# A hybrid decoder trunk on one core: small float32r products put ahead of float32 ones within a batch, and an early first activation

## The chip, the cores and the metric

The kernel runs on one core of a Trainium2 chip. The metric is the device time of one execution in microseconds (us); lower is better. Engines are named as the profile names them: PE is TensorE's matrix unit, PEld its weight loads, DVE is VectorE, ACT is ScalarE, POOL is GpSimd, SP issues the DMAs.

## The reference

Two layers over 528 tokens (16 learned meta tokens and 512 real ones) of width 1024, in float32. Cut to what matters here:

```
for l in range(DEPTH):                          # DEPTH = 2
    proj = rms_norm(h, norm1_g[l]) @ w_in[l]    # z, xbc, dt, q, k, v, gate logits
    y_ssd = ssd_mixer(z, xbc, dt, ...)          # conv, silu, chunked state-space scan, gated group norm
    y_attn = sliding_window_attention(q, k, v, ...)   # window 128, meta keys, sinks
    merged = g_ssd * (y_ssd @ w_ssd_down[l]) + g_attn * (y_attn @ w_attn_down[l])
    h = h + merged @ w_o[l]
    h = h + square(relu(rms_norm(h, norm2_g[l]) @ w_mlp_up[l])) @ w_mlp_down[l]
return h[:, 16:]
```

## The kernel before

Everything is held transposed, with features on the 128 partitions and tokens along the free dimension. Each large matrix product ("dense", L545) works through 128x128 weight tiles. For accuracy a float32 value is split into a high and a low float32r part (whi and wlo for weights, hnh and hnl for the normalised rows), and three float32r products replace one float32 product: high by high, low by high, high by low. These dense products have 264, 266 or 512 columns and fill most of PE's time.

Besides them there is a large number of small products. Those of attention (L1064) are scores (k2h and k2l by q, two pairs of products at a time) and probabilities by values (ar by vt or vm): both are float32r. Between the two, attention transposes its probabilities (cst by at, L442), which is a float32 operation on PE. All other small products are float32: the state-space chunks (L1228: transposes cst by xb, then btk by xdd, xdt by gm, st by xb), the norms (cst by zs, one column each; cst by rg) and the rotary norms (cst by au, two columns).

The small work is written as generators. Each "yield" ends a stage and names what the next stage needs: "ps" is a free PSUM bank, "pe" says only that the stage issues products, "ar" is a buffer of probabilities. A planner (class Flow) keeps an estimated clock for every engine while the program is being built. After every second dense product it calls "tick" (L265). If the last batch of small products is at least GAP = 3600 ns of its clock ago (the flag open_), tick may issue products; stages that use only DVE, ACT, POOL or SP may be issued at any time. It goes through the queues w, post, misc, tail, chunk, attn in this order and takes the first stage that is ready by its estimates. A stage taken is written into the program at once, and each engine executes its instructions in the order written. So the order of the instructions on each engine is what the planner decides, and the estimated clock has no other effect on the chip.

At the start, SP loads the first parameters, the first row block of h, two weight tiles of v (wraw, 512 KB each), the weights of dt (rawdt), and then the other rows. ACT scales h into hgh, casts the three weights into wvh, and PE's first products wait for these casts. ACT's function table is loaded by an instruction that the compiler puts ahead of ACT's first activation.

Of the kernel before, what the change touches and what calls it, by code (L numbers as in the profile page):

```python
# [9 lines left out]
F32 = mybir.dt.float32  # L10
F32R = mybir.dt.float32r
I32 = mybir.dt.int32
AF = mybir.ActivationFunctionType
# [4 lines left out]
P = 128  # L18
# [62 lines left out]
class Ring:  # L81
# [5 lines left out]
    def at(self, k=1):  # L87
        return sorted(self.free)[k - 1]
# [8 lines left out]
class Task:  # L97
# [3 lines left out]
    def at(self, flow):  # L101

        t = self.ready
        for k, n in self.needs.items():
            if k == "if":
                if not n():
                    return INF
            elif k == "after":
                if not all(x.done for x in n):
                    return INF  # L110
                t = max([t] + [x.end for x in n])
            elif k == "data":
                aps = n()
                if aps is None:
                    return INF
                t = max(t, flow.there("pe", (), aps))
            elif k == "bank":
                t = max(t, flow.rings["ps"].at(n))
            elif k != "pe":
                t = max(t, flow.rings[k].at(n + (flow.SPARED if k == "ps" else 0)))  # L120
        return t


class Flow:
# [52 lines left out]
    def there(self, e, outs, ins):  # L177

        t = 0.0
        for aps, out in ((ins, False), (outs, True)):  # L180
            for ap in aps:
                bank = ap.space == PSUM
                p0, p1, f0, f1 = self.box(ap)
                for log in (self.written, self.read) if out or bank else (self.written,):
                    for q0, q1, g0, g1, at, e_ in log.get(ap.tensor.name, ()):

                        if e_ != e if bank and e_ else False:
                            hit = True
                        else:
                            hit = (out or log is self.written) and q0 < p1 and p0 < q1 and g0 < f1 and f0 < g1  # L190
                        if hit:
                            t = max(t, at + self.HOP.get((e_, e), 130.0))
        return t
# [71 lines left out]
    def tick(self):  # L265


        begin = self.t["pe"]
        open_ = begin - self.batch >= self.GAP
        for _ in range(24):  # L270
            if self.busy():
                break
            now = self.t["pe"]
            calm = max(self.t["v"], self.t["s"]) - now < self.CALM
            for t, q in self.active():
                if not open_ and any(k in ("pe", "ps", "bank") for k in t.needs):
                    continue
                if (calm or q is not self.queues["attn"]) and t.at(self) <= now:
                    self.step(t, q)
                    break  # L280
            else:
                break
        if self.t["pe"] > begin:
            self.batch = self.t["pe"]

    def wait_any(self):

        best = None
        for t, q in self.active():
            at = t.at(self)  # L290
            if at < INF and (best is None or at < best[0]):
                best = (at, t, q)
        assert best is not None, "nothing can go on"
        self.step(best[1], best[2])
# [68 lines left out]
def hybrid_trunk_kernel(ctx: ExitStack, tc: tile.TileContext, h0, params, consts, rope, wdt, w, out,  # L363
# [7 lines left out]
    sm = ctx.enter_context(tc.tile_pool(name="sm", bufs=2))  # L371
# [5 lines left out]
    S = Engine(F, "s", nc.scalar)  # L377
    G = Engine(F, "g", nc.gpsimd)
# [12 lines left out]
    class Slot:  # L391
# [12 lines left out]
        def free(self, at=None):  # L404
            F.rings[self.kind].free[self.j] = max(F.end, F.t["pe"] if at is None else at)
# [8 lines left out]
    def unit(name, dt=F32):  # L414
        return un.tile([P, 4, UW], dt, name=name, tag="u")
# [17 lines left out]
    def mm(o, lhsT, rhs, start=True, stop=True):  # L433
        n = Engine.size(rhs)
        if rhs.dtype == F32R and n >= 256:
            cost = n / 2.4
        else:
            cost = max(n, 128) * 4 / 2.4 * (0.66 if o.shape[0] == 64 else 1.0)
        F.run("pe", cost, [o], [lhsT, rhs], PE.matmul(out=o, lhsT=lhsT, rhs=rhs, start=start, stop=stop))  # L439

    def transpose(o, in_, k=P):
        F.run("pe", 108.0 if in_.shape[1] > 64 else 60.0, [o], [in_], PE.transpose(out=o, in_=in_, identity=C("ident", k)[:, :k]))  # L442
# [246 lines left out]

    h = Rows("h", KD)  # L690
    F.dma(par[:, 0, 0:KD], params[:, 0, 0:KD])
    few = CCOL["low"][0]
    wvt.open(0)
    tasks_ = [x for x, q in F.active()]
# [38 lines left out]
    for l in range(depth):  # L733
# [174 lines left out]
        for c in range(5):  # L908
            ps = banks[c]
# [154 lines left out]
        def attention(n, kv):  # L1064
# [29 lines left out]
            def score(i):  # L1094
                ps = Slot("ps")
                for x in range(2):
                    mm(ps.t[:, :kw], q2[:, i, :], k2[x][:, kv, k0:k0 + kw], start=(x == 0), stop=(x == 1))
                return ps

            def top(i, ps):  # L1100
                col = (4 * a + i) * 2 + hb
                V.tensor_tensor_reduce(out=pt[i], in0=ps.t[:nq, :nk], in1=mask,
                                       scale=rqk[:nq, n, col:col + 1], scalar=sk[:, i:i + 1],
                                       op0=ALU.add, op1=ALU.max, accum_out=mx[:nq, i:i + 1])
                ps.free()

            for i in range(0, 4, 2):
                yield {"ps": 2}
                two = [score(i), score(i + 1)]
                yield  # L1110
                top(i, two[0])
                top(i + 1, two[1])
# [13 lines left out]
            def piece(p):  # L1126

                o, kk, cc = pieces[p]
                need = {"ps": 1, "ar": 1}
                if not po:  # L1130
                    need["ps"], need["po"] = 2, 1
                yield need
                if not po:
                    po.append(Slot("ps"))
                    turn.append(Slot("po"))
                s_, pp = Slot("ar"), Slot("ps")
                if kk < P <= nq:

                    for i in range(4):
                        transpose(pp.t[0:32, i * nq:(i + 1) * nq], pt[i][:, o:o + 32], nq)  # L1140
                    if p == len(pieces) - 1:
                        p_.free()
                    yield
                    h_ = slice(s_.j * 1024, s_.j * 1024 + 4 * nq)
                    S.copy(ar[0:32, h_], pp.t[0:32, :4 * nq])
                    yield
                    V.tensor_tensor(out=ar[32:64, h_], in0=pp.t[0:32, :4 * nq], in1=ar[0:32, h_], op=ALU.subtract)
                    pp.free()
                    yield {"pe": 1}
                    mm(po[0].t[:, :4 * nq], vm[:, kv].rearrange("p x d -> p (x d)"), ar[:, h_],  # L1150
                       start=(p == 0), stop=(p == len(pieces) - 1))
                    s_.free()
                    return
                for i in range(4):
                    transpose(pp.t[:kk, i * nq:(i + 1) * nq], pt[i][:, o:o + kk], nq)
                if p == len(pieces) - 1:
                    p_.free()
                yield
                ph, pl_ = (ar[:kk, s_.j * 1024 + z:s_.j * 1024 + z + 4 * nq] for z in (0, 512))
                S.copy(ph, pp.t[:kk, :4 * nq])  # L1160
                yield
                V.tensor_tensor(out=pl_, in0=pp.t[:kk, :4 * nq], in1=ph, op=ALU.subtract)
                pp.free()
                yield {"pe": 1}
                for x, r in enumerate((ph, pl_)):
                    mm(po[0].t[:, :4 * nq], (vt[:, cc - 1, kv] if cc else vm[:kk, kv]).rearrange("p x d -> p (x d)"), r,
                       start=(p == 0 and x == 0), stop=(p == len(pieces) - 1 and x == 1))
                s_.free()


            live = [piece(p) for p in range(len(pieces))]
            wait, t = {}, 0
            started = 1
# [30 lines left out]
        def put_attention(qt, a):  # L1204
            F.put("misc", q_rms(qt, a))
            for n in range(c_first, 5):
                for kv in (2 * a, 2 * a + 1):
                    att.append(F.put("attn", attention(n, kv)))
# [4 lines left out]
        ar = unit("ar", F32R).rearrange("p r t -> p (r t)")  # L1213
# [580 lines left out]
```

## Time and profile before

| | us |
|---|---|
| median of 3 runs (2354.28, 2356.80, 2356.81) | 2356.8 |
| the profiled execution, its own time | 2351.39 |
| its span, first to last instruction | 2349.5 |
| PE busy in the span | 2322.6 |
| POOL busy | 1327.6 |
| DVE busy | 1186.7 |
| ACT busy | 1027.7 |

The profiled execution is a fourth execution of the same program; 1.9 us of its time lie outside its span. The four executions lie 5.4 us apart. Busy time is the union of the engine's instructions, so for PE it also holds time in which products run slowly.

### The profile page before, as it was taken

Reading aid. Unit: us, or ns where it says so; the run is one execution under the profiler, and the core shown is the slowest. Engines: PE = TensorE matmul, PEld = TensorE weight load, DVE = VectorE, ACT = ScalarE, POOL = GpSimd, SP = SyncE. Lnnn points to the kernel's source line nnn. Section 1 sums busy time; section 2 is a strip of 40 time slices with the busy share of each in tenths; the row PEclk is TensorE's granted clock in tenths of the full one; section 3 lists DMA queues with packets and bytes.
Section 4 is the critical chain, followed back from the end, with each engine's and each line's share of the span. In section 5 each row is a group of like instructions: output and inputs, shape, how many; then the busy total and the mean of one; then the engine's idle time right before and its main releaser. Section 6 shows DMA issues by size and latency. Waiting matters only on the chain.

```text
span 2349.5 us, 41761 instructions
## 1 busy us (share of the span) xinstructions
PE 2322.6 (99%) x16038; PEld 2129.6 (91%) x16038; DVE 1186.7 (51%) x2511; ACT 1027.7 (44%) x2007; POOL 1327.6 (57%) x1733
## 2 busy tenths in 40 slices
PE   8999999999999999999999999999999999999999
PEld 8899999999999999999998888999887888888887
DVE  7687688888422322122146876888873223222121
ACT  5455566666422333223244555656563223423221
POOL 6555545566555555555557555565575555555554
PEclk9999999999999999999999999999999999999999
DMA  4233334433443322222243333333434433222222
GB/s 167 85 93 103 106 105 116 109 93 99 136 165 114 132 81 91 90 91 91 97 141 99 104 103 109 112 104 104 116 104 154 148 113 135 90 99 90 99 98 99
DMA packets 133588, 257.41 MB, mean 110 GB/s; under 512 B 16470, under 2 KB 66318, under 8 KB 133390
## 3 DMA queue, kind: packets, MB, share of 16 engines
q1 hardware_dynamic: 133390, 254.75, 34.5%
q8 instruction: 127, 2.08, 0.4%
q14 instruction: 71, 0.58, 0.1%
HBM read 232.03 MB, written 17.33 MB: 106 GB/s over the span
## 4 chain that ended last, share of the span: by engine, by line
PE 92%; DVE 4%; ACT 1%; POOL 1%; issue 1%; DMA 1%; SPq 0%; ACTq 0%; DVEq 0%; POOLq 0%
PE ps L439 90%; PE ps L442 3%; DVE rqs L356 1%; DVE at L356 1%; DVE xh L356 0%; POOL wlo L356 0%; DVE xb L356 0%; DMA gm<-ac_dram 0%; ACT gm L356 0%; ACT whi L356 0%; DVE raw L356 0%; DVE ar L356 0%; DVE gm L356 0%; DVE qa L356 0%; SPq L232 0%
## 5 line engine op out<-in xcount | busy, mean ns | idle before, releaser
L356 POOL TENSOR_TENSOR wlo<-wraw,whi 128x256 fp32r<-128x256 f32 x1272 | 988.7, 809 | 747.1 <-ACT whi L356 732.9
L356 ACT CAST whi<-wraw 128x1024 fp32r<-128x1024 f32 x340 | 355.6, 1046 | 725.0 <-PE ps L439 692.1
L439 PE MATMUL ps<-hnh,whi 128*128 128x266 f32 (+2 forms) x1984 | 371.7, 305 | 0.0
L439 PE MATMUL ps<-hnl,whi 128*128 128x266 f32 (+2 forms) x1984 | 369.5, 305 | 0.0
L439 PE MATMUL ps<-hnh,wlo 128*128 128x266 f32 (+2 forms) x1984 | 365.6, 304 | 0.0
L439 PEld LDWEIGHTS ps<-hnl,whi 128*128 128x128 f32 x1984 | 293.0, 189 | 13.4
L439 PEld LDWEIGHTS ps<-hnh,wlo 128*128 128x128 f32 x1984 | 291.6, 189 | 13.2
L439 PEld LDWEIGHTS ps<-hnh,whi 128*128 128x128 f32 x1984 | 292.0, 189 | 12.6 <-issue 0.3
L356 DVE SCALAR_TENSOR_TENSOR h<-ps,h 128x264 f32<-128x264 f32 (+1 forms) x120 | 62.1, 518 | 324.4 <-PE ps L439 324.4
L439 PE MATMUL ps<-hgh,wlo 128*128 128x264 f32 (+1 forms) x832 | 165.0, 320 | 0.3 <-POOL wlo L356 0.3
L439 PE MATMUL ps<-hgl,whi 128*128 128x264 f32 (+1 forms) x832 | 164.5, 319 | 0.4 <-DVE hgl L356 0.4
L439 PE MATMUL ps<-hgh,whi 128*128 128x264 f32 (+1 forms) x832 | 164.1, 319 | 0.0
L439 PE MATMUL ps<-hidl,whi 128*128 128x264 f32 (+1 forms) x768 | 152.6, 320 | 0.0
L439 PE MATMUL ps<-hidh,whi 128*128 128x264 f32 (+1 forms) x768 | 152.5, 320 | 0.0
L439 PE MATMUL ps<-hidh,wlo 128*128 128x264 f32 (+1 forms) x768 | 152.5, 320 | 0.0
L356 DVE SCALAR_TENSOR_TENSOR tmp<-ps,rbc 128x264 f32<-128x264 f32 (+1 forms) x96 | 49.3, 515 | 183.7 <-PE ps L439 162.3
L439 PEld LDWEIGHTS ps<-hgh,wlo 128*128 128x128 f32 x832 | 128.6, 190 | 11.5 <-POOL wlo L356 0.5
L439 PEld LDWEIGHTS ps<-hgl,whi 128*128 128x128 f32 x832 | 128.5, 189 | 11.6 <-DVE hgl L356 0.6
L439 PEld LDWEIGHTS ps<-hgh,whi 128*128 128x128 f32 x832 | 128.7, 190 | 11.2
L439 PE MATMUL ps<-y,whi 128*128 128x264 f32 (+1 forms) x768 | 137.0, 320 | 0.0
L439 PEld LDWEIGHTS ps<-hidl,whi 128*128 128x128 f32 x768 | 118.8, 188 | 11.1
L439 PEld LDWEIGHTS ps<-hidh,wlo 128*128 128x128 f32 x768 | 118.7, 188 | 11.1
(217 smaller groups left out, 3904.0 us busy)
## 6 DMA issues: line engine op xcount, KB each, us to landing
wraw<-w_dram SPq DMA_DIRECT2D x344, 512.0 KB, 3.2
gm<-ac_dram SPq DMA_DIRECT2D x64, 256.0 KB, 5.0
et<-ac_dram SPq DMA_DIRECT2D x128, 64.0 KB, 4.7
t<-au SPq DMA_DIRECT2D x48, 66.0 KB, 2.8
h<-h_dram SPq DMA_DIRECT2D x8, 264.0 KB, 4.7
at<-rope_dram SPq DMA_DIRECT2D x4, 528.0 KB, 4.8
y_dram<-xb SPq DMA_DIRECT2D x4, 528.0 KB, 5.2
yr<-y_dram SPq DMA_DIRECT2D x8, 264.0 KB, 4.5
```

Of the source, the lines that this page charges most:

```text
L356: inst = fn(*a, **k)
L439: F.run("pe", cost, [o], [lhsT, rhs], PE.matmul(out=o, lhsT=lhsT, rhs=rhs, start=start, stop=stop))
L442: F.run("pe", 108.0 if in_.shape[1] > 64 else 60.0, [o], [in_], PE.transpose(out=o, in_=in_, identity=C("ident", k)[:, :k]))
```

## The change

It has two parts. First, tick no longer takes the first ready stage. It looks at all ready stages and takes the one of lowest rank: rank 0 is a stage without products, 1 is a stage with float32r products only, 2 a stage that has float32r products and the transposes of attention, 3 a stage of float32 products. Attention's stages carry a mark "r" for this, which has no other use. Second, a one-column activation on a zeroed tile z is written ahead of everything else on ACT.

```diff
             now = self.t["pe"]
             calm = max(self.t["v"], self.t["s"]) - now < self.CALM
+            best = None
             for t, q in self.active():
-                if not open_ and any(k in ("pe", "ps", "bank") for k in t.needs):
-                    continue
-                if (calm or q is not self.queues["attn"]) and t.at(self) <= now:
-                    self.step(t, q)
-                    break
-            else:
+
+                rank = 0
+                if any(k in ("pe", "ps", "bank") for k in t.needs):
+                    rank = 3 if "r" not in t.needs else 2 if "ar" in t.needs else 1
+                    if not open_:
+                        continue
+                if ((best is None or rank < best[0]) and (calm or q is not self.queues["attn"])
+                        and t.at(self) <= now):
+                    best = (rank, t, q)
+            if best is None:
                 break
+            self.step(best[1], best[2])
...
     F.dma(par[:, 0, 0:KD], params[:, 0, 0:KD])
+
+    z = sm.tile([P, 1], F32, name="z", tag="z")
+    G.memset(z, 0.0)
+    S.activation(out=z, in_=z, func=AF.Square)
...
-                yield {"ps": 2}
+                yield {"ps": 2, "r": 1}
...
-                    yield {"pe": 1}
+                    yield {"pe": 1, "r": 1}
...
-                yield {"pe": 1}
+                yield {"pe": 1, "r": 1}
```

On ACT, at the very start of the program, these rows stood (hgh is the scaled row block, wvh the cast weights of v and dt):

```order
L356 ACT_TABLE_LOAD
L356 ACTIVATE hgh_106<-h_80,par 128x528
L356 CAST wvh<-wraw 128x7x128
L356 CAST wvh_84<-wraw 128x128
L356 CAST wvh<-wraw 128x7x128
```

With the change there are these; line numbers are six higher here:

```order
L362 ACT_TABLE_LOAD
L362 ACTIVATE z<-z 128x1
L362 ACTIVATE hgh_109<-h_80,par 128x528
L362 CAST wvh<-wraw 128x7x128
L362 CAST wvh_87<-wraw 128x128
L362 CAST wvh<-wraw 128x7x128
```

The table load stands first in both; what follows it is now an activation that needs only z, so the load's wait is no longer that for h.

On PE, the first place at which the two programs differ is a batch in the query projections of layer 1 (cst by au is a rotary norm, cst by at a transpose of attention, k2h and k2l by q are scores; hnh, hnl are dense). Before:

```order
L439 MATMUL ps<-hnh_160,whi 128x264 x2
L439 MATMUL ps<-cst,au 128x2 x5
L442 MATMUL ps<-cst,at_952 16x16 x4
L439 MATMUL ps<-k2h,q_1290 128x256
L439 MATMUL ps<-k2l,q_1290 128x256
L439 MATMUL ps<-k2h,q_1290 128x256
L439 MATMUL ps<-k2l,q_1290 128x256
L439 MATMUL ps<-hnl_162,whi 128x264 x2
```

With the change:

```order
L445 MATMUL ps<-hnh_163,whi 128x264 x2
L445 MATMUL ps<-k2h,q_1293 128x256
L445 MATMUL ps<-k2l,q_1293 128x256
L445 MATMUL ps<-k2h,q_1293 128x256
L445 MATMUL ps<-k2l,q_1293 128x256
L445 MATMUL ps<-cst,au 128x2 x5
L448 MATMUL ps<-cst,at_955 16x16 x4
L445 MATMUL ps<-hnl_165,whi 128x264 x2
```

The scores moved from the end of the batch to its head, next to the dense float32r products.

On DVE, the same stretch of the program (at and mx are the scores with their maxima, rqk and qa the rotary norm, ar the low part of the probabilities). Before:

```order
L356 TENSOR_SCALAR rqk<-ps 128x5x2
L356 TENSOR_TENSOR qa_549<-qa_549,t_1332 128x528
L356 TENSOR_TENSOR ar<-ps,ar 16x64
L356 ISA at_952,mx<-ps,cst,par,rqk 128x144
L356 ISA mx 128x1
L356 ISA at_952,mx<-ps,cst,par,rqk 128x144
L356 ISA mx 128x1
L356 TENSOR_SCALAR mx<-mx 128x4
```

With the change:

```order
L362 TENSOR_SCALAR mx<-mx 128x4
L362 TENSOR_TENSOR es<-par,mx 128x4
L362 TENSOR_SCALAR rqk<-ps 128x5x2
L362 TENSOR_TENSOR qa_552<-qa_552,t_1335 128x528
L362 TENSOR_TENSOR su<-su,es 128x4
L362 RECIPROCAL su<-su 128x4
L362 TENSOR_SCALAR at_955<-at_955,su 128x144 x4
L362 TENSOR_TENSOR ar<-ps,ar 16x64
```

The work on the scores now comes ahead of the rotary norm and ahead of ar.

Counted over the whole program, the products are the same 15,190 in both, and between their dense neighbours they form 220 batches before and 221 now. A run of float32 products, with float32r ones on both sides, occurs 252 times before and 216 times now. In 39 batches before, float32 products stood both ahead of and behind float32r ones; now in 7. In 33 they stood only ahead; now in 1. In 19 they stood only behind; now in 84. On PE the order is the same in the two programs up to the batch shown, from 640.62 us to 1314 us of the trace of before, and from 1813.43 us to the end; it differs from 116.28 to 640.62 us and, but for a short piece, from 1314 to 1813.43 us.

## Rows read from the trace of the kernel before

**Rows 1.** Page, busy time, share of the span and instructions, PE.

```profile
PE 2322.6 (99%) x16038; PEld 2129.6 (91%) x16038; DVE 1186.7 (51%) x2511; ACT 1027.7 (44%) x2007; POOL 1327.6 (57%) x1733
```

**Rows 2.** Windows, the two reordered stretches: from:to, length, busy per engine, clock, DMA.

```profile
116.28:640.62 524.34, 522.96 (x4293) 500.60 (x4292) 398.01 (x950) 312.58 (x751) 296.60 (x388) 1.00 0.38 105
1348.19:1813.43 465.24, 461.43 (x3100) 408.63 (x3099) 338.83 (x754) 266.10 (x585) 276.41 (x357) 1.00 0.39 111
```

**Rows 3.** Waits of PE in 1348.19:1813.43: waited for, us in total, times, longest.

```profile
PE ps L442 <- POOL rg L356: 1.5, 1, 1.5
PE ps L439 <- DVE ar L356: 1.4, 2, 0.8
```

**Rows 4.** Timeline, ACT and PE at the start: start us, us, what.

```profile
5.03 1.28 ACT L356 ACT_TABLE_LOAD   x1 [5.03 <-DMA h<-h_dram]
6.33 0.73 ACT L356 ACTIVATE hgh<-h,par 128x528 fp32r<-128x528 f32 x1
...
6.97 0.92 ACT L356 CAST wvh<-wraw 128x896 fp32r<-128x896 f32 x1
...
7.99 0.93 ACT L356 CAST wvh<-wraw 128x896 fp32r<-128x896 f32 x1
...
9.46 2.86 PE L439 MATMUL ps<-wvh,hgh 128*128 128x288 f32 x10 [9.46 <-ACT wvh L356]
```

**Rows 5.** Issue of the second weight tile (timeline, SP), and its us to landing (DMA).

```profile
2.12 0.43 SPq L232 DMA_DIRECT2D wraw<-w_dram  x1
...
wraw<-w_dram SPq DMA_DIRECT2D x1, 512.0 KB, 5.4
```

**Rows 6.** Timeline of PE, one batch with two float32 runs (413.86 to 416.40).

```profile
413.28 0.40 PE L439 MATMUL ps<-hnl,whi 128*128 128x264 f32 x2
413.52 0.41 PE L439 MATMUL ps<-hnh,wlo 128*128 128x264 f32 x2
413.86 0.66 PE L439 MATMUL ps<-gm,xdt 128*64 128x128 f32 x8
...
415.46 0.60 PE L442 MATMUL ps<-cst,at 128*128 128x128 f32 x4
415.81 0.37 PE L439 MATMUL ps<-k2h,q 128*128 128x272 f32 x1
416.02 0.29 PE L439 MATMUL ps<-k2l,q 128*128 128x272 f32 x1
...
416.40 0.77 PE L439 MATMUL ps<-hnh,whi 128*128 128x264 f32 x5
```

**Rows 7.** The same forms elsewhere without a switch (timeline), and one transpose's mean (lines).

```profile
195.31 0.66 PE L439 MATMUL ps<-gm,xdt 128*64 128x128 f32 x8
...
196.54 0.66 PE L439 MATMUL ps<-gm,xdt 128*64 128x128 f32 x8
...
218.33 0.63 PE L439 MATMUL ps<-ar,vt 128*128 128x512 f32 x2
...
219.29 0.89 PE L439 MATMUL ps<-hnh,whi 128*128 128x266 f32 x6
...
L442 PE MATMUL ps<-cst,at 128*128 128x128 f32 x224 | 33.5, 272 | 0.0
```

**Rows 8.** Timeline, first and last of seven batches with ar late: DVE and PE.

```profile
389.77 0.66 PE L439 MATMUL ps<-gm,xdt 128*64 128x128 f32 x8
389.99 0.69 DVE L356 TENSOR_TENSOR ar<-ps,ar 128x512 fp32r<-128x512 f32 x1
...
1715.21 0.68 DVE L356 TENSOR_TENSOR ar<-ps,ar 128x512 fp32r<-128x512 f32 x1
1715.33 0.59 PE L439 MATMUL ps<-xdd,btk 128*128 128x256 f32 x2
```

**Rows 9.** Windows of PE alone: from:to, length, busy (count), granted clock, DMA.

```profile
835.00:841.90 6.90, 6.90 (x34) 0.51 0.22 76
841.90:848.00 6.10, 6.10 (x50) 1.00 0.24 78
```

More of the change, by code (lines that the diff above doesn't have):

```diff
@@ L118, in at @@
                 t = max(t, flow.rings["ps"].at(n))
-            elif k != "pe":
+            elif k not in ("pe", "r"):
                 t = max(t, flow.rings[k].at(n + (flow.SPARED if k == "ps" else 0)))
```

## The prediction

> **What bounds the kernel now.** I read the page first, then the windows by stage, the waits and the timeline of PE. The page has PE busy for 99% of the span, DVE, POOL and ACT for 44 to 57% [rows 1]. So time is won only by what PE doesn't have to do, or doesn't have to wait for. A busy share hides slow products, so the second look is at the clock and at start-to-start times. The third is at the two stretches in which the change reorders the products, 116.28 to 640.62 us and about 1348 to 1813.43 us; elsewhere PE's order stays. In them PE is busy 522.96 of 524.34 us and 461.43 of 465.24 us [rows 2]. What it sits idle there is 1.4 + 3.8 = 5.2 us: seven waits, of which the longest are for POOL's rg (1.5 us) and DVE's ar (two, 1.4 us together) [rows 3]. That is all that a better order could win from waiting. PE's whole idle time is 2349.5 - 2322.6 = 26.9 us; 9.46 us of it are the start [rows 4], and the other 12.2 us lie where the order stays, the end of the program among them.
>
> **The early activation.** The load of ACT's table stands at 5.03 us, behind the landing of h, and takes 1.28 us; the scaling of h starts 0.02 us after it [rows 4]. With z it waits for one small memset of POOL and lies in time in which ACT had nothing to do, so its own 1.28 us are hidden by the wait for h. Behind it the scaling of h moves to about 5.05 us. But PE's first product waits for the casts of three weights, and the second large cast, at 7.99 us [rows 4], needs the second weight tile. That was issued at 2.12 us and landed 5.4 us later, at about 7.5 us [rows 5]. So this cast moves from 7.99 to about 7.55 us at the earliest, and PE's start by some 0.4 us, not 1.28. The ends are 0 (if the first tile lands only just before its cast at 6.97 us, which the rows can't exclude) and 1.28 us. I take 0.4 us, since the second tile's landing is the latest event that a row shows. What follows on PE is paced by PE itself, so the 0.4 us should stay.
>
> The Trainium skill has another price for the load: "ScalarE: Activation LUTs", in What ACT_TABLE_LOAD costs, gives about 1.28 us for the load and 1.38 us for a drain, 2.66 us together. The load here agrees; the drain doesn't show, as the next activation starts 0.02 us behind the load. By the page 2.66 us would leave ACT's chain, by the row 1.28 us; the landing of the weight tile lets through no more than 0.4 us of either.
>
> **The order within a batch.** The products are the same, so the direct gain is the number of switches saved times the price of one. The float32 runs between float32r products go from 252 to 216: 36 round trips fewer. Is there a price? Single rows suggest one: four transposes start at 415.46, the score behind them at 415.81, and the next score comes 0.21 us later, where such scores otherwise follow each other at 0.12 to 0.13 us [rows 6, 7]. That is 0.08 us at an edge, and it looks the same at the other edge, so 0.17 us for a round trip. But the other side must be counted too: four transposes take 4 x 0.109 = 0.44 us (four of them last 0.60 us, and one 0.272 us, so they start (0.60 - 0.272) / 3 = 0.109 us apart), and here the next product starts after 0.35 us, 0.09 us early [rows 6, 7]. The edge only shifts a start. The whole batch tells it. It has two float32 runs. From 413.52 to 416.40 us are 2.88 us. Its parts, from places without such switches: two dense products 0.24 us (413.28 to 413.52), gm and st products 1.23 us (195.31 to 196.54), two products of ar and four scores 0.96 us (218.33 to 219.29), four transposes 0.44 us; in sum 2.87 us [rows 6, 7]. So two round trips cost 0.01 us. I take 0.01 us for one and 0.03 us as the upper end (the rounding of these starts): 36 x 0.01 = 0.4 us, at most 1.1 us.
>
> **What the order does to waits.** A product that moves to the head of a batch loses the time that the float32 products ahead of it gave to its operands. I compared, for the 81 batches of before in which a float32r run has float32 products ahead of it, when the operands of its first float32r stage were ready and when the batch began. In 74 they were ready before the batch began, so the move costs nothing. In seven, ar came from DVE later than that: in the first, DVE ends it at 390.68 us and the batch begins at 389.77; in the last at 1715.89 against 1715.33 [rows 8]. If all seven went straight to the head, PE would wait 4.5 us in sum, and part of that it waits already. The planner doesn't put a stage there that it holds for not ready, so the cost lies between 0 and 4.5 us. In return float32 stages move back and their operands (rg, at, xdd) get more time: between 0 and the 3.8 us that PE now waits for others than these ar (5.2 - 1.4, [rows 2, 3]). Behind a product in PE's queue stands the whole dense stream, so each such wait counts in full. I put the two against each other at zero net. The stages without products go first in both engines' favour or not: DVE works in order, and what comes forward (scores, at) pushes something else back (the rotary norm, ar). DVE is busy 398 of 524 us in layer 1's stretch [rows 2], so a stage of it that is pushed back has about a quarter of the time to be caught up. I see no sign for this and leave it at zero, with the scatter below.
>
> **The sum.** -0.4 (start) - 0.4 (switches) + 0 (waits) = -0.8 us, with single ends of -1.3 and 0, -1.1 and 0, -5.2 and +4.5. The profiled execution took 2351.39 us, of which 2349.5 us are span, so the changed kernel would take 2350.6 us beside it. The four executions of before run from 2351.39 to 2356.81 us, with a mean of 2354.8 and a median of the three runs of 2356.8; less 0.8 these are 2354.0 and 2356.0. I predict 2355 us, between the two. A difference under 0.2% (4.7 us) can't be told from none here.
>
> **Rivals.**
> 1. The waits go: if the new order removes all 5.2 us of waiting in the two stretches, the sum is -6.0 us, or 2349.8 us. For it: the longest of them are for float32 products, which move back. Against it: any new order has its own near misses, and the planner's estimates, which were off by up to 1.5 us there [rows 3], are the same. Chance 0.17.
> 2. Slower: float32r products at the head of batches meet DVE's ar too early. At 4.5 us for the seven batches the sum is +3.7 us, still no difference. It decides from 5.5 us of new waits (4.7 + 0.8), which is nine batches at the mean of 0.65 us. With twice the seven it is 9 us, sum +8.2 us, 2363 us. For it: 84 batches now begin with float32r products where 19 did. Against it: 74 of 81 have slack. Chance 0.15.
> 3. A switch does cost 0.17 us, as the rows at its edges look: 36 x 0.17 = 6.1 us, sum -6.5 us, 2349 us. Against it stands the whole batch of [rows 6]. Chance 0.05.
> 4. The early activation wins all of its 1.28 us, because the weight tiles land earlier than in this one execution: 0.9 us more, which changes no class. It is within the forecast.
>
> What would cost more than a wait is a fall of the clock. From 835.0 to 841.9 us the granted clock was 0.51, the lower of its two levels (1.2 GHz); 34 products took 6.9 us there, where 50 take 6.1 us just after [rows 9], so about 6.9 - 34 x 0.122 = 2.8 us were lost. Ahead of it PE had waited and then run one-column products. The new order makes no float32 run much longer than before, so I expect no new fall; one more would add 2.8 us to rival 2.
>
> **How the numbers follow.** The forecast has 0.63. Of it I give 0.02 to either side for the scatter of the medians. Faster by over 0.2%: 0.17 + 0.05 + 0.02 = 0.24. Slower: 0.15 + 0.02 = 0.17. Same: 0.59. The range reaches from rival 3 and a low median (2347 us) to rival 2 (2363 us); outside I leave 0.1 on either side.
>
> **What would show it.** Right: the table load before 3 us and PE's first product at about 9.05 us; the busy time of PE in the two stretches within 1 us of 985 us; waits in them of 3 to 8 us in sum, with other names. Wrong: PE's first product at 8.2 us (then the landing was not the bound); busy time down by 6 us with the same products (a switch has a price); a list of waits for ar that adds up to over 10 us, or a further stretch at the low clock. If the time falls by more than 6 us, something outside the three terms was moved.

## The result, and the profile after

The changed kernel takes 2366.8 us (median of 4 runs, 2365.55 to 2368.62) against 2356.5 us for the kernel before on the same chip (4 runs): a ratio of 1.0052, 95% interval 1.0040 to 1.0064. It is 10.3 us slower, outside the forecast range of 2347 to 2363 us.

The start went as described. In the timeline of the changed kernel (start us, us, engine, line, instruction; in brackets how long the engine sat idle and for what) the table load no longer waits for h [rows 4]:

```profile
0.73 1.28 ACT L362 ACT_TABLE_LOAD   x1 [0.73 <-PEq L1792]
2.03 0.20 ACT L362 ACTIVATE z<-z 128x1 f32<-128x1 f32 x1
4.64 0.73 ACT L362 ACTIVATE hgh<-h,par 128x528 fp32r<-128x528 f32 x1 [2.41 <-DMA h<-h_dram]
...
7.63 1.14 ACT L362 CAST wvh<-wraw 128x896 fp32r<-128x896 f32 x2 [0.63 <-DMA wraw<-w_dram]
...
9.10 1.33 PE L445 MATMUL ps<-wvh,hgh 128*128 128x288 f32 x4 [9.10 <-ACT wvh L362]
```

The loss is in layer 1's stretch. PE's order is the same outside the two reordered stretches, so the same products can be found in both traces. The windows of the changed kernel (from:to, length, busy per engine with counts, granted clock, DMA) over the products of [rows 2]:

```profile
118.14:661.33 543.19, 531.94 (x4295) 506.60 (x4294) 398.04 (x951) 311.53 (x750) 295.17 (x379) 0.99 0.37 101
1369.71:1830.84 461.13, 460.61 (x3100) 409.10 (x3099) 338.80 (x760) 265.05 (x585) 267.50 (x347) 1.00 0.39 112
```

Layer 1's stretch grew from 524.34 to 543.19 us, 18.85 us more. PE's idle time in it went from 524.34 - 522.96 = 1.4 us to 543.19 - 531.94 = 11.25 us, which is 9.9 us of the growth; its busy time for the same products grew by 9.0 us. Layer 2's stretch became 4.1 us shorter: there most of the waits of [rows 3] went, and 0.5 us of idle time is left. Where the order stays, this execution is 1.9 us longer up to the first reordered batch (116.28 us before, 118.14 us now), where it has a fall of the clock that the profile before lacks and the control e6, with the order of before, has too. It is 0.8 us longer between the layers and 0.1 us shorter behind them. The sum is the 17.3 us by which the two spans differ; the profiled execution before was among the faster ones and this one is the slowest of four, so the medians differ by less.

The waits of PE in layer 1's stretch (waited for: us in total, times, longest):

```profile
PE ps L445 <- DVE q L362: 4.1, 2, 2.5
PE ps L445 <- DVE ar L362: 3.7, 4, 2.0
PE ps L445 <- POOL xdd L362: 1.7, 1, 1.7
PE ps L445 <- ACT ar L362: 1.2, 1, 1.2
PE ps L445 <- DVE zs L362: 0.5, 1, 0.5
```

Before, only these two stood there:

```profile
PE ps L439 <- DVE ar L356: 0.7, 1, 0.7
PE ps L442 <- DVE at L356: 0.6, 1, 0.6
```

In layer 2's stretch these are left of [rows 3]:

```profile
PE ps L445 <- POOL xdd L362: 0.2, 1, 0.2
PE ps L448 <- POOL rg L362: 0.2, 1, 0.2
```

Most of the growth of the busy time is the clock. In windows of PE alone (length, busy with count, granted clock, DMA) four stretches at the lower level (1.2 GHz) follow waits, and the second is shown beside the window behind it:

```profile
252.60:256.00 3.40, 3.40 (x23) 0.50 0.28 42
262.85:266.30 3.45, 3.45 (x16) 0.51 0.20 78
266.30:269.70 3.40, 3.40 (x28) 1.00 0.43 154
423.27:426.70 3.43, 3.43 (x21) 0.50 0.40 51
614.42:617.80 3.38, 3.38 (x15) 0.50 0.55 90
```

About 3.4 us at half the clock cost at most 1.7 us each, 6.8 us for the four. The rest of the 9.0 us is placed with e5 below.

What the waits are for is read one engine further back. Of the five kinds, the waits for q and for ar have a cast on ACT ahead of them. The waits of ACT in the same stretch have this row for the state-space chunk's activations of gm, whose input SP loads from DRAM:

```profile
ACT gm L362 <- DMA gm<-ac_dram: 34.0, 16, 4.6
```

Before it was 9.4 us in 12 waits:

```profile
ACT gm L356 <- DMA gm<-ac_dram: 9.4, 12, 2.3
```

The timeline of the longest wait of PE shows how it comes through (SPq is the issue of a transfer):

```profile
253.57 0.38 SPq L232 DMA_DIRECT2D gm<-ac_dram  x1
...
258.95 1.28 ACT L362 ACTIVATE gm<-gm,acs 128x128 f32<-128x128 f32 x4 [3.81 <-DMA gm<-ac_dram]
...
261.13 0.61 ACT L362 CAST q<-qa 64x512 fp32r<-64x512 f32 x1
261.77 0.59 ACT L362 CAST ar<-ps 128x512 fp32r<-128x512 f32 x1
261.78 0.69 DVE L362 TENSOR_TENSOR q<-qa,q 64x512 fp32r<-64x512 f32 x1 [4.86 <-ACT q L362]
262.50 0.69 DVE L362 TENSOR_TENSOR ar<-ps,ar 128x512 fp32r<-128x512 f32 x1
262.52 0.39 PE L445 MATMUL ps<-k2h,q 128*128 128x272 f32 x1 [2.52 <-DVE q L362]
```

The transfer is issued at 253.57 us and ACT stands before its landing from 255.1 to 258.95 us. Behind it in ACT's order are the casts of q and ar, behind these DVE's low parts, and behind those the score products, which now stand at the head of a batch. PE waits 2.52 us for them, and the clock falls right behind.

Theory 1 was this chain alone: stages without products first put gm's activations on ACT too early. Theory 2 was rival 2 of the prediction: float32r stages at the heads of batches. Theory 3: any new order has near misses of its own.

### The profile page after: what moved, and what is told of

Read it like the earlier page. It is cut to its first block, busy times and chain, and to the rows that moved or that the text cites. A ratio compares the mean times of both kernels' runs of the same rounds, so it can differ in the third digit from the quotient of the medians.

```text
span 2366.8 us, 41750 instructions
## 1 busy us (share of the span) xinstructions
PE 2333.1 (99%) x16038; PEld 2138.6 (90%) x16038; DVE 1184.4 (50%) x2514; ACT 1026.8 (43%) x2008; POOL 1322.8 (56%) x1726
## 4 chain that ended last, share of the span: by engine, by line
PE 91%; DVE 3%; DMA 2%; ACT 1%; POOL 1%; issue 1%; SPq 0%; DVEq 0%; POOLq 0%; ACTq 0%
PE ps L445 88%; PE ps L448 2%; DMA gm<-ac_dram 1%; DVE raw L362 1%; DVE rqs L362 1%; ACT gm L362 1%; SPq L232 0%; DVE at L362 0%; DVE xb L362 0%; DMA t<-au 0%; DMA wraw<-w_dram 0%; POOL wlo L362 0%; ACT whi L362 0%; DVE ar L362 0%; POOL k2l L362 0%
## 5 line engine op out<-in xcount | busy, mean ns | idle before, releaser
L445 PE MATMUL ps<-hnh,wlo 128*128 128x266 f32 (+2 forms) x1984 | 371.3, 307 | 0.0
L362 DVE SCALAR_TENSOR_TENSOR raw<-ps,half,raw 128x262 f32<-128x262 f32 (+3 forms) x294 | 143.2, 490 | 40.1 <-ACT raw L362 32.7
L445 PEld LDWEIGHTS ps<-hgh,whi 128*128 128x128 f32 x832 | 128.0, 189 | 11.1
L445 PEld LDWEIGHTS ps<-hidh,wlo 128*128 128x128 f32 x768 | 118.8, 188 | 11.1
```

Source lines behind the costliest of these rows:

```text
L362: inst = fn(*a, **k)
```

## The experiments

Each was timed beside the kernel before on the same chip; ratios are to that, with 95% intervals. A ratio of 1.0052 is the changed kernel's.

**Which of the two rules.** e2 keeps rank 0 for stages without products, but has no order of float32r and float32 (stages that take a place in the ring ar come last):

```diff
-                    rank = 3 if "r" not in t.needs else 2 if "ar" in t.needs else 1
+                    rank = 2 if "ar" in t.needs else 1
```

> The early activation and the stages without products first, but no order between float32r and float32 stages (stages that take a place in the ring ar come last, the others keep their queue order). Theory 1, the chunk's activations of gm stand on ScalarE ahead of attention's casts and wait there for their transfer: the loss stays, 2363 to 2369 us, and in layer 1's stretch ScalarE waits over 25 us in sum for gm's transfer (34.0 after the change, 9.4 before). Theory 2, float32r stages at the heads of batches come too early for their ar: no loss, 2355 to 2358 us. Theory 3, any new order has near misses of its own: a time anywhere from 2350 to 2368 us, not tied to ScalarE's waits for gm.

Measured: 2353.8 us, 0.9998 (0.9989 to 1.0007). ACT's wait for gm over the program is 34.1 us, more than the 24.5 us of before, and nothing is lost. In layer 1's stretch it is 23.8 us, more than twice the 9.4 us of before, though under the 25 us that theory 1 named. So theory 1 as it was put falls: in this order, early activations of gm on ACT do no harm by themselves.

e3 takes stages without products in queue order, as before, and only prefers float32r among stages with products:

```diff
-                if ((best is None or rank < best[0]) and (calm or q is not self.queues["attn"])
+                if ((best is None or 0 < rank < best[0]) and (calm or q is not self.queues["attn"])
                         and t.at(self) <= now):
                     best = (rank, t, q)
+                    if rank == 0:
+                        break
```

> The early activation and float32r ahead of float32 among the stages with products, but stages without products taken in the order of the queues, as before the change. Theory 1: the loss is gone, 2354 to 2358 us, ScalarE's waits for gm's transfer in layer 1's stretch near the 9.4 us of before. Theory 2: the loss stays, 2363 to 2369 us. Theory 3: anywhere from 2350 to 2368 us.

Measured: 2375.9 us, 1.0087 (1.0073 to 1.0101), above the range of every theory. The loss is here, and larger. The longest waits of PE from 115 to 665 us are for four kinds of work of DVE and POOL, not for ar alone:

```profile
PE ps L447 <- DVE ar L364: 3.8, 5, 2.2
PE ps L450 <- POOL rg L364: 3.4, 2, 2.2
PE ps L447 <- POOL xdd L364: 2.6, 3, 1.3
PE ps L450 <- DVE gm L364: 2.3, 1, 2.3
```

**What the wait for gm costs.** e5 keeps the changed kernel's order on PE, ACT, DVE and POOL instruction for instruction. The planner sees the old operands, the chip gets others:

```diff
-                F.dma(gm[:, :, :n], ac_dram[hs, 0, t0:t0 + n]...)
...
+                F.dma(gm[:, :, :n], ac_dram[hs, 0, t0:t0 + n]...,
+                      gd[:, :, :n4], ac_dram[hs, 0, t0:t0 + n4]...)
...
-                    S.activation(out=gm[:n, i, :n], in_=gm[:n, i, :n], func=AF.Relu, ...)
+                    F.run("s", n / 1.2 + 86.0 + 93.0, [gm[:n, i, :n]], [gm[:n, i, :n], bias],
+                          nc.scalar.activation(out=gm[:n, i, :n], in_=C("up", n)[:, :n], func=AF.Relu, ...))
```

> The changed kernel with the same order on PE, ScalarE, VectorE and GpSimd, but the first activations of gm read a constant that lies in SBUF, and the transfer brings a quarter of its columns into a tile that nobody reads: the chunk's decay is left out of the result. Only ScalarE's wait for gm's transfer is gone. Theory 1: PE's waits at 182.8, 262.5, 556.3 and 558.0 us go (6.5 us in sum) and with them one or two falls of the clock (1.7 us each): 2356 to 2361 us. Theory 2: within 1.5 us of the changed kernel, 2365 to 2368 us. Theory 3: as theory 2, or a loss spread over many engines of which this takes 1 to 4 us, 2363 to 2366 us.

Measured: 2346.7 us, 0.9965 (0.9952 to 0.9977): 8.5 us under before, where the changed kernel is 10.3 us over it. That is under the range of every theory. These 19 us are more than the whole loss. The window over the same products:

```profile
116.62:639.16 522.54, 522.54 (x4296) 500.53 (x4294) 396.99 (x951) 310.90 (x750) 296.04 (x379) 1.00 0.34 93
```

Layer 1's stretch fell from 543.19 to 522.54 us. PE has no wait left in it, not even those for POOL's xdd and DVE's zs that have no cast of attention ahead of them, and no fall of the clock. Since PE's order is the same in both, the start of every product can be set beside that in the changed kernel. Of the 20.65 us that the changed kernel slips in this stretch, 12.7 us come at its nine waits, of which 11.1 us are idle time and the rest counts as busy; 5.9 us come in the four falls, and 2 us elsewhere. In the changed kernel, the chain that ended last has 2% of DMA, and the page gives 1% to gm's transfer; the second line is that of e5, with 0% of DMA:

```profile
PE 91%; DVE 3%; DMA 2%; ACT 1%; POOL 1%; issue 1%; SPq 0%; DVEq 0%; POOLq 0%; ACTq 0%
```

```profile
PE 97%; DVE 1%; POOL 1%; ACT 1%; DMA 0%; issue 0%; SPq 0%; DVEq 0%; POOLq 0%; ACTq 0%
```

e6 is the control, the same edit in the kernel before:

> The kernel before, in its own order on PE, ScalarE, VectorE and GpSimd, with the first activations of gm reading a constant as in e5_gm_resident (the chunk's decay is left out). The control for that run, which was 20 us faster than the changed kernel. Theory 1 (the order decides what ScalarE's waits for gm's transfer cost: little before, 20 us after): 2346 to 2352 us, 4 to 9 us under the kernel before. Theory 2 (float32r stages at the heads of batches cost by themselves): the kernel before has few of them late, so 2353 to 2356 us, no change. Theory 3 (what a smaller transfer brings, alike in any order): 20 us faster than before, 2333 to 2338 us.

Measured: 2352.5 us, 0.9989 (0.9981 to 0.9998), 2 us less than before and between the ranges of theories 1 and 2.

```profile
118.82:643.14 524.32, 523.01 (x4294) 500.69 (x4293) 398.92 (x950) 311.58 (x751) 296.40 (x388) 1.00 0.34 93
```

Layer 1's stretch has 524.32 us, where it had 524.34 [rows 2]. So the same kind of wait, 9.4 us of it on ACT, costs PE nothing there in the order of before, and 20.65 us in the changed one, where it is 34.0 us on ACT. In this order the whole edit brings 2 us, so a smaller transfer as such brings no more here. What it brings by itself in the changed order was not run.

e7 is the edit in e3:

> float32r first alone, as in e3_f32r_only and in its order, with the first activations of gm reading a constant (the chunk's decay is left out). If the loss is made of both, float32r stages at the heads of batches and their casts behind gm's wait on ScalarE, it goes with the wait: 2344 to 2352 us against 2375.9. If float32r first costs by itself through other waits (POOL's xdd and rg, VectorE's ar), most of it stays: 2365 to 2375 us.

Measured: 2360.5 us, 1.0026 (1.0015 to 1.0036). It is 6.0 us over before, where e3 was 20.7: about 15 us go with the wait and 6 us stay, between the two ranges: DVE's ar (2.2 us at one place) and POOL's xdd (2.5 us) are late without it.

**Whether the wait can be planned away.** e4 adds 2 us to the planner's landing of gm. The planner has 1100 + 728 + 1400 ns = 3.2 us from issue to landing for these 256 KB; the page of before has a median of 5.0 us.

```diff
+                F.note("sp", [gm[:, :, :n]], [], F.t["dma"] + 3400.0)
```

> The changed kernel, but the planner takes gm's transfer to land 2 us later than it did, so that the activations of gm are issued later on ScalarE. Theory 1: ScalarE's wait for gm's transfer in layer 1's stretch falls from 34.0 to under 15 us, PE's waits behind it (6.5 us in the changed kernel) and a fall of the clock go, 2357 to 2361 us. Theory 2: within 2 us of the changed kernel, 2365 to 2369 us. Theory 3: the wait for gm falls, and the time goes anywhere from 2350 to 2368 us, since the order is new again.

Measured: 2380.8 us, 1.0106 (1.0092 to 1.0120), the slowest of all and above the range of every theory. ACT's wait for gm did fall, from 45.1 to 15.7 us over the program. PE waits for others instead, from 115 to 665 us:

```profile
PE ps L445 <- DVE xh L362: 4.3, 1, 4.3
PE ps L445 <- ACT ar L362: 2.0, 1, 2.0
PE ps L445 <- POOL rg L362: 1.5, 1, 1.5
```

e10 writes the activations of gm, and their product with cb, behind the chunk's first products and its state, so that the transfer has that time to land; e11 is the same in the kernel before:

```diff
-                for i in range(4):
-                    S.activation(out=gm[:n, i, :n], in_=gm[:n, i, :n], func=AF.Relu, ...)
...
                 st[c] = nst
             if not need_y:
                 mid.free()
             else:
+                yield
+                for i in range(4):
+                    S.activation(out=gm[:n, i, :n], in_=gm[:n, i, :n], func=AF.Relu, ...)
...
```

> The changed kernel, with the chunk's activations of gm (and their product with cb) written behind the chunk's first products and its state, so that the transfer has those stages' time to land; the result is the whole one. If ScalarE's wait for gm's transfer is what makes the loss: ScalarE waits under 5 us for it in all (45.1 in the changed kernel) and the time is 2346 to 2354 us. If a new order draws its own near misses whatever ScalarE waits for: anywhere from 2350 to 2380 us with the wait gone. If the new place makes the last products of a chunk wait for gm: PE waits on VectorE's gm, over 2360 us.

> The same edit in the kernel before. Its wait for gm's transfer cost 2 us (e6_before_gm_resident), so at most that is to be won: 2351 to 2355 us if ScalarE's wait is the cause; anywhere from 2350 to 2380 us if the order draws its near misses otherwise.

Measured: e10 2360.8 us, 1.0033 (1.0021 to 1.0045); e11 2351.5 us, 0.9992 (0.9983 to 1.0000). In both ACT waits for gm's transfer nowhere. In e10 that leaves a loss of 7.9 us, where the change has 10.3; PE's new longest waits are for DVE's gm (2.6 us) and POOL's rg (2.1 us). Taking the wait away in a fixed order (e5) brings it all, taking it away by a new order brings part or nothing. So theory 1 alone can't be the whole.

**Whether it is the draw.** The next runs keep every rule and shift a number of the planner, so that another order comes out: the two delays of a ready stage (LAT and LATP, 100 ns) or the least distance of batches (GAP, 3600 ns).

```diff
-    LAT = 100.0
-    LATP = 100.0
+    LAT = 110.0
+    LATP = 110.0
```

> The kernel before with the planner's two delays for a ready stage at 110 ns instead of 100: nothing that should matter, but a new order (2405 of PE's 15192 places differ). Theory 3, every new order draws its own near misses: 2348 to 2370 us, off by over 5 us. Theories 1 and 2, only the change's rules move stages to where they meet a wait: 2353 to 2359 us.

> The changed kernel with the same delays at 110 ns (3353 of PE's 15192 places differ). Theory 3: anywhere from 2348 to 2380 us, off the changed kernel by over 5 us. Theories 1 and 2: 2363 to 2372 us, since the rules are the same.

> The changed kernel with batches at least 3.5 us apart instead of 3.6. If the rules make the loss in most orders: 2360 to 2375 us. If the order drawn makes it (the delay of 110 ns took it away): anywhere from 2350 to 2380 us, and the time goes with the number of falls of PE's clock in the two stretches with small products (1.7 us each) and with PE's waits there.

> The changed kernel with batches at least 3.7 us apart. The same two cases as with 3.5: 2360 to 2375 us if the rules make the loss in most orders, anywhere from 2350 to 2380 us if the drawn order makes it.

> The kernel before with batches at least 3.5 us apart instead of 3.6. If its rules leave slack behind attention's casts in most orders: 2351 to 2360 us. If any order draws its near misses, the rules aside: anywhere from 2350 to 2380 us, as the changed kernel did (2374.2 with 3.5 us).

> The kernel before with batches at least 3.55 us apart: another order by the same rules. Same two cases: 2351 to 2360 us if the rules of before leave slack, anywhere from 2350 to 2380 us if not.

> The changed kernel with the planner's delays at 90 ns instead of 100. If the changed rules are slower in most orders: 2360 to 2375 us; if 100 ns drew a bad order by chance: as likely 2350 to 2358 us, as with 110 ns (2352.3).

> float32r first alone, as in e3_f32r_only (2375.9 us), with the planner's delays at 110 ns: a second order by that rule. If float32r first is the part that takes attention's slack: 2360 to 2380 us. If 2375.9 was the draw: 2348 to 2356 us, like the orders by the rules of before.

The table has all the orders that compute everything, without e4, e10 and e11. The waits are PE's and ACT's (for gm's transfer), summed from 110 to 1900 us.

| kernel | us | ratio, 95% interval | PE waits, us | ACT for gm, us |
|---|---|---|---|---|
| rules of before, as it stood | 2353.0 to 2356.5 | 1 | 8.1 | 24.5 |
| e8, 110 ns | 2352.7 | 1.0002 (0.9993 to 1.0010) | 7.8 | 23.5 |
| e14, GAP 3500 | 2353.1 | 0.9989 (0.9980 to 0.9998) | 6.3 | 35.0 |
| e15, GAP 3550 | 2348.0 | 0.9979 (0.9971 to 0.9988) | 5.2 | 22.9 |
| e2, other engines first | 2353.8 | 0.9998 (0.9989 to 1.0007) | 6.0 | 34.1 |
| e3, float32r first | 2375.9 | 1.0087 (1.0073 to 1.0101) | 21.1 | 41.8 |
| e18, float32r first, 110 ns | 2372.3 | 1.0072 (1.0055 to 1.0089) | 18.0 | 32.4 |
| both rules, the change | 2366.8 | 1.0052 (1.0040 to 1.0064) | 15.4 | 45.1 |
| e9, both, 110 ns | 2352.3 | 0.9992 (0.9983 to 1.0001) | 8.1 | 29.2 |
| e12, both, GAP 3500 | 2374.2 | 1.0090 (1.0075 to 1.0105) | 19.6 | 46.1 |
| e13, both, GAP 3700 | 2364.0 | 1.0040 (1.0028 to 1.0052) | 11.5 | 30.7 |
| e16, both, 90 ns | 2377.4 | 1.0095 (1.0081 to 1.0109) | 20.7 | 42.3 |

The time goes with PE's waits, and not with ACT's waits for gm: 35.0 us of those do no harm in e14 (11.0 us of them in layer 1's stretch, where the change has 34.0). Of the seven orders with float32r first, six lose 0.4 to 1.0%; of the five without, none loses. (e4 and e10, which have float32r first too, lose; e11, which has not, doesn't.) So theory 3 holds in part: the draw decides by 25 us what the change costs, and 10 ns decide the draw. But the float32r rule makes the bad draws likely, and that is theory 2. Of the rule "other engines first" alone there is one order only, so its share is known less well.

e19 takes gm's wait out of the slowest of these orders, e16:

> The changed kernel with delays at 90 ns (2377.4 us) in the same order, with the first activations of gm reading a constant, as in e5_gm_resident (the chunk's decay is left out). If ScalarE's wait for gm's transfer makes the loss in this order too: 2345 to 2355 us. If other waits carry it here (PE waits 6.8 us for GpSimd's xdd and 4.3 us at one place for ScalarE's whi): 2362 to 2375 us.

Measured: 2356.2 us, 1.0007 (0.9998 to 1.0016). Of e16's loss of 21.6 us 1.2 us are left, so over 20 us go with the wait; the time is 1.2 us above the first range put down. PE's waits for POOL's xdd are among what goes; the long one for ACT's whi stays. The first two lines are from e16, from 110 to 1900 us, the third from e19, where no wait for xdd is left:

```profile
PE ps L445 <- POOL xdd L362: 6.8, 3, 4.3
PE ps L445 <- ACT whi L362: 5.1, 2, 4.3
```

```profile
PE ps L445 <- ACT whi L362: 4.3, 2, 3.5
```

So a wait that the profile puts down to xdd can begin at gm's transfer, an engine or two further back.

**The early activation alone:**

> The kernel before with the early activation alone: all engines keep their order. The prediction's first term: PE's first product 0.4 us earlier in the profile (9.05 against 9.46 us), the time 0.4 us less, which is less than this measurement tells apart; 2353 to 2356 us. The rival that the whole table load of 1.28 us is won: 1.3 us less.

Measured: 2355.0 us, 0.9997 (0.9989 to 1.0006): no difference that can be told. PE's first product is at 8.95 us in this trace.

## Why the prediction was wrong

**Start: right in size, and smaller than its scatter.** The table load went from 5.03 to 0.73 us, and PE began at 9.10 us, forecast 9.05. ACT's second large cast still waited for its weight tile, as the prediction said of the bound. But the landings vary by as much as the gain: e14 begins at 8.79 us without the early activation, e5 at 9.49 us with it. The page "ScalarE: Activation LUTs" (What ACT_TABLE_LOAD costs) of the Trainium skill adds a drain of about 1.38 us to the load, for a switch to another set of functions. Here, at the only load of the program, z starts 0.02 us behind the load, so no drain shows.

**Switches: no price seen.** In layer 2's stretch, at full clock in both, PE is busy 460.61 us where it was 461.43. That is 0.8 us for 17 of the 36 round trips, and part of it may belong to the waits that went. In layer 1's stretch, with another 17, e5 has the new order without waits: 522.54 us where before had 522.96 [rows 2]. That is 1.2 us for 34 of the 36, near the upper end of 1.1 us that the prediction gave, and rival 3's 6.1 us are out.

**Waits: the step that failed.** The sum had zero net, with ends of -5.2 and +4.5 us. Idle time of PE in the two stretches went from 5.2 to 11.25 + 0.5 = 11.8 us, 6.6 us more. The prediction's own signs were 3 to 8 us of waits if it was right, and a further stretch at the low clock if it was wrong. The sentence that failed is "In 74 they were ready before the batch began, so the move costs nothing." It took the times at which q and ar were ready from the trace of before and moved only the products. It was a slack count in one execution of one order, and what fills ACT and DVE ahead of the casts is reordered as well. The 3.8 us that it set against this, as waits for others than ar, held another 0.7 us for ar in layer 1's stretch, so they were 3.1 us. Counted in the traces of layer 1's stretch, from the end of the DVE instruction that writes the low part of ar or q to the first product that reads that part:

| kernel | batches that begin with float32r, of all | ar and q ready under 0.5 us ahead, of all |
|---|---|---|
| before | 19 of 92 | 2 of 53 |
| e2, other engines first | 23 of 87 | 9 of 60 |
| changed | 56 of 94 | 10 of 56 |
| e3, float32r first | 58 of 94 | 10 of 55 |

Close arrivals alone don't make the loss: e2 has nearly as many and PE waits 2.7 us in that stretch, against 11.2 us with the change and 14.9 us in e3. What sets the last two apart in this table is how many batches begin with float32r. My reading is that products at the head leave the casts no batch in front to hide in, so that lateness of ACT reaches PE, and ACT waits up to 4.6 us where gm's activations stand ahead of their transfer's landing. The rule takes the slack; the transfer, which lands 1.8 us later than planned (5.0 against 3.2 us), uses it up. That the transfer is what uses it up is shown by e5, e19 and most of e7; that the heads take the slack is argued, from the seven orders against five. So the loss is rival 2 (2363 us, chance 0.15) with the right place and a cause of the lateness that the prediction did not look for: it read PE's waits in those stretches, and never ACT's, which had 9.4 us of gm's waits to show. e2 shows the other half of the step, "I see no sign for this and leave it at zero" for stages without products first, to be right as far as one order tells.

**The clock: the second part of the loss.** The step "so I expect no new fall" was wrong: there are four new ones in layer 1's stretch, about 6 of the 9.0 us of added busy time with the same products. It had priced one at 2.8 us, from a fall of 6.9 us; these last about 3.4 us and cost at most 1.7 us each, but there are four. The reason given, float32 runs not longer than before, looked at the products and not at the waits ahead of them; the new falls lie behind new waits, and with the waits gone in e5 none is left in that stretch.

**Layer 2** went as rival 1: of 3.8 us of waits 0.5 are left, and the stretch is 4.1 us shorter by the same rules, in this one order.

Open is why 110 ns draws an order that loses nothing (e9), with gm's waits of 29.2 us on ACT and 54 of 95 batches in layer 1's stretch that begin with float32r. Open is also how much of the 6 us that stay in e7 belongs to which engine.

The only complete version here that is over 0.2% faster than the kernel before is e15, that kernel with GAP at 3550 ns: 2348.0 us. It is a better draw by the rules of before; no run shows it to be a better rule.

## What to carry to other kernels

Where an in-order engine feeds the bound engine, moving a consumer to the head of the queue can spend its slack; read what the feeding engine waits for (its DMA waits above all), not only when its results were ready in the old order. To price a suspected wait, keep the order of all engines and make the waiting instruction read resident data: that told 19 us from 2 us where reorderings only drew new numbers. And a change to a scheduler's rule is judged over several orders, with a number shifted by a hair, and not by the one that it happens to draw.

## What the runs showed that was not expected

A wait of PE needn't be long for the clock to fall behind it, and a longer one needn't bring a fall. In the changed kernel PE waited 0.51 us at 612.67 us and 1.67 us at 250.91 us and ran at 0.50 soon after; 1.61 us at 182.77 us, and 1.15 and 1.21 us at 556.32 and 558.03 us, brought none. The wait of 0.51 us was followed by ten one-column products before the clock fell. And 10 ns in two constants of the planner, with no rule touched, moved the time from 2366.8 to 2352.3 us; 10 ns the other way moved it to 2377.4 us.
